# Every large SBUF tile starts at a multiple of 512 bytes: a two-layer encoder on one Trainium2 core

## The chip, the cores and the metric

One core of one Trainium2 chip runs the whole program. The metric is the device time of one execution in microseconds (us). Three executions of the kernel before took 2646.51, 2648.54 and 2650.86 us; the median, 2648.54 us, is the time before. Engines are named as in the profile: PE multiplies matrices, PEld loads its stationary operand, DVE and ACT work on vectors, POOL is a slower helper, and SP issues nearly all DMAs.

## The reference

Two groups of tokens (512 and 256, together T = 768 columns) pass through the same two layers and a final RMSNorm, all in float32 with D = 1024:

```python
x = x + 0.5 * swiglu(rmsnorm(x, f1_n), f1_g, f1_u, f1_d)      # 1024 -> 2816 -> 1024
x = x + mixer(rmsnorm(x, mix_n), ...)                         # layer 0: gated MLP beside windowed
...                                                           # attention; layer 1: 2-D neighbourhood attention
x = x + 0.5 * swiglu(rmsnorm(x, f2_n), f2_g, f2_u, f2_d)
```

So there are six phases: l0f1, l0m, l0f2, l1f1, l1m, l1f2. The four feed-forward phases (FFNs) take three quarters of the time.

## The kernel before

**How a product is made.** Activations lie transposed: 128 features on the partitions, tokens along the row. Each float32 operand is split into a high and a low float32r part, and `mm3` (L175) adds three matmuls in PSUM: high by high, low by high, high by low. All of PE's matmuls of this kind are recorded at L139 in `mmul`. Weights arrive as `raw` tiles of 128 rows of 4,096 bytes (`raw`, L91, issued by SP), and `wsplit` (L103) makes `whi` on ACT (L113) and `wlo` on DVE (L114). `whi` and `wlo` are then the stationary operand, 128 columns at a time; the activation tile (`b11` to `b22`, `d`, `xh`, `xl`, `oh`, `ol`) is the moving operand, mostly 384 columns of 4 bytes, so 1,536 bytes in each partition. In the profile a matmul stands as `ps<-moving,stationary`.

**An FFN.** `ffn` (L416) uses Strassen's scheme on halves of the tokens and of the features, with seven products in place of eight. The gate and up products of a pair of 128 hidden features are 7 products x 2 names x 4 slices x 3 = 168 matmuls that move the `b11`, `b21`, `t1`, `t2`, `t3`, `n4`, `b22` tiles (I call them b tiles; 56 of them, in the pool `comb`). There are 11 pairs: 1,848 such matmuls for each FFN. `down` (L628) multiplies the hidden features back: 84 matmuls for a pair that move `db`, `dt`, `dn` tiles, and `down_last` (L693) another 192 with `dh` (d tiles, in the pool `work`). The order of PE is written out by hand; the other engines follow a scheduler with semaphores for each tile.

**Where tiles lie.** A partition of SBUF has 229,376 bytes. Tiles are placed when the program is built: sizes are padded to 32 bytes, and a pool opened on the left or right side grows from that end. On the left end, in bytes: 2,176 are taken before the program's own tiles; `ident`, `ones`, `onesr` 3 x 512; `gains`, `ngains` 2 x 224; eight `x` tiles of 3,072; four `raw` of 4,096; ten `whi`/`wlo` of 2,048; `acc` 3,072; three `nt` of 1,536; and the norms' small tiles `sm`, `smi`, `yh`, `yl`, together 480. So `x`, `raw`, `whi`, `wlo`, `acc` and `nt` all start 64 bytes past a multiple of 512, and the first tile of the left side stands at 73,760 = 144 x 512 + 32. The right side ends at 229,344 = 447 x 512 + 480. The big pools follow in tiles of 1,536, 2,048 or 3,072 bytes, all multiples of 512. So **every b, d, xh, xl, oh or ol tile that lies on the left starts 32 past a multiple of 512, and on the right 480 past one.**

The side changes with the phase (`open` L80, `other` L771, `mixer_tiles` L774, `ffn_open` L303):

| phase | stretch of the profile, us | b tiles or xh, xl, oh, ol | d tiles |
|---|---|---|---|
| l0f1 | 0 to 523 | right (480) | left (32) |
| l0m | 523 to 782 | right (480) | - |
| l0f2 | 782 to 1283 | left (32) | right (480) |
| l1f1 | 1283 to 1772 | left (32) | right (480) |
| l1m | 1772 to 2132 | left (32) | - |
| l1f2 | 2132 to 2647 | right (480) | left (32) |

Counted in the built program, 11,980 matmuls move 384 columns over all 128 rows: 5,880 from a start of 480 with a stationary operand at 64, 5,880 from 32 with one at 64, 96 from 480 with one at 480, 96 from 32 with one at 32 (the last two are `dh` with the kept weights `khi`, `klo`), and 28 others. Another 2,216 move 256 or 512 columns over 128 rows, in the mixers, from starts of 32, 64, 448 or 480.

Of the kernel before, what the change touches and what calls it, by code (L numbers as in the profile page):

```python
# [9 lines left out]
F32 = mybir.dt.float32  # L10
F32R = mybir.dt.float32r
BF16 = mybir.dt.bfloat16
I32 = mybir.dt.int32
# [3 lines left out]
P = 128  # L17
D = 1024
KD = D // P
# [9 lines left out]
NORMS = ("l0_ffn1_norm", "l0_mix_norm", "l0_ffn2_norm", "l1_ffn1_norm", "l1_mix_norm", "l1_ffn2_norm", "final_norm")  # L29
# [9 lines left out]
NMASK = 8 * (24 + 32 + 24) + 4 * (40 + 40)  # L39
# [12 lines left out]
class Trunk:  # L52
# [4 lines left out]
    def __init__(self, ctx, tc, aps, phases=PHASES):  # L57
        self.tc, self.nc, self.aps, self.phases = tc, tc.nc, aps, phases
        self.units = []
        self.woff = self.pi = 0  # L60
        self.t = 0.0
        self.chains = []
        self.spare = []
        self.first = []
        self.copied = []
        pool = lambda name, bufs, **kw: ctx.enter_context(tc.tile_pool(name=name, bufs=bufs, **kw))
        self.cp = pool("const", 1)
        self.xp = pool("x", 1)
        self.rawp = pool("raw", 4)
        self.wp = pool("w", NW)  # L70
        self.np_ = pool("norm", 1)
        self.mm = pool("mm", 4, space=bass.MemoryType.PSUM)
        self.aux = pool("aux", 4, space=bass.MemoryType.PSUM)
        self.dram = pool("spill", 1, space=bass.MemoryType.DRAM)
        self.guards = {}
        self.side = "left"
# [147 lines left out]
    def norm_tok(self, acc, c0, c1):  # L224

        nb = (c1 - c0) // P
        ps = self.psum(self.aux, "aux")
        for b in range(nb):
            self.mmul(ps[:, b : b + 1], acc[:, c0 + b * P : c0 + (b + 1) * P], self.ones[:, 0:1], True, True)
        sm = self.np_.tile([P, 3, 6], F32, tag="sm", name="sm", bufs=3)  # L230
        it = self.np_.tile([P, 6], I32, tag="smi", name="smi", bufs=2)
        y = sm[:, 1, :nb]
        self.rsqrt(y, ps[:, :nb], 1.0 / D, sm[:, 0, :nb], sm[:, 2, :nb], it[:, :nb])
        return y

    def norm_spread(self, y, pool=None):

        nc = self.nc
        yh = self.np_.tile([P, 3], F32R, tag="yh", name="yh", bufs=2)
        yl = self.np_.tile([P, 3], F32, tag="yl", name="yl", bufs=2)  # L240
        nc.vector.tensor_copy(yh, y)
        nc.vector.tensor_tensor(out=yl, in0=y, in1=yh.bitcast(F32), op=ALU.subtract)
        rb = self.psum(self.aux, "aux")
        for i, t in enumerate((yh.bitcast(F32), yl)):
            diag = (
                pool.tile([P, H], F32R, tag="diag", name="diag", bufs=2)
                if pool and i
                else self.np_.tile([P, H], F32R, tag="nt", name="diag", bufs=3)
            )
            for b in range(3):  # L250
                c = slice(b * P, (b + 1) * P)
                if i:
                    nc.scalar.activation(diag[:, c], self.ident, AF.Copy, scale=t[:, b : b + 1])
                else:
                    nc.vector.tensor_scalar(
                        out=diag[:, c], in0=self.ident, scalar1=t[:, b : b + 1], scalar2=None, op0=ALU.mult
                    )
            self.mmul(rb[:, :H], self.onesr, diag, i == 0, i == 1)
        return rb[:, :H]
# [637 lines left out]
    def finish_rows(self, pool, n, ps_list, outs, adds, init, sink=None):  # L897


        nc = self.nc  # L900
        st = pool.tile([P, 4, 8], F32, tag="st", name="st", bufs=3)
        mx, nm, sm, ri = (st[:, i, :] for i in range(4))
        for i in range(n):
            nc.vector.tensor_tensor_reduce(  # L904
                out=outs[i], in0=ps_list[i], in1=adds[i], scale=1.0, scalar=init[i],
                op0=ALU.add, op1=ALU.max, accum_out=mx[:, i : i + 1],
            )
        nc.vector.tensor_scalar(out=nm[:, :n], in0=mx[:, :n], scalar1=-1.0, scalar2=None, op0=ALU.mult)  # L908
        for i in range(n):
            nc.scalar.activation(  # L910
                outs[i], outs[i], AF.Exp, bias=nm[:, i : i + 1], accum_out=sm[:, i : i + 1]
            )
        if sink is not None:
            nc.vector.tensor_tensor(out=ri[:, :n], in0=sink, in1=nm[:, :n], op=ALU.add)
            nc.scalar.activation(ri[:, :n], ri[:, :n], AF.Exp)
            nc.vector.tensor_tensor(out=sm[:, :n], in0=sm[:, :n], in1=ri[:, :n], op=ALU.add)
        nc.vector.reciprocal(ri[:, :n], sm[:, :n])
        for i in range(n):
            nc.vector.tensor_scalar(  # L919
                out=outs[i], in0=outs[i], scalar1=ri[:, i : i + 1], scalar2=None, op0=ALU.mult  # L920
            )


    def mixer0(self):
        nc = self.nc
        mp = self.mixer_open("m0")
# [7 lines left out]
                nc.sync.dma_start(t[:, c0:c1], self.aps["rope"][i, :, : c1 - c0])  # L934
        msk = mp.tile([P, 3 * P], F32, tag="msk", name="msk")
        nc.sync.dma_start(msk, self.aps["gmask"])
        sink = mp.tile([P, 8], F32, tag="sink", name="sink")
        nc.sync.dma_start(sink, self.aps["sink"].partition_broadcast(P))
        lng = mp.tile([P, 512], F32, tag="lng", name="lng")
        nc.sync.dma_start(lng, self.aps["ln_g"].partition_broadcast(P))  # L940
# [231 lines left out]
    def mixer1(self):  # L1172
        nc = self.nc
        mp = self.mixer_open("m1")
# [1 line left out]
        xs = (self.xh, self.xl)  # L1176
        self.xcols = lambda k, c0, c1: (self.xh[k][:, c0:c1], self.xl[k][:, c0:c1])
        TE = TA + 64
        mb = mp.tile([P, NMASK], BF16, tag="mb", name="mb")
        for i in range(0, NMASK, 512):  # L1180
            n = min(512, NMASK - i)
            mf = mp.tile([P, 512], F32, tag="tb", name="mf")
# [224 lines left out]

    def build(self):
        nc = self.nc
        self.ident = self.cp.tile([P, P], F32, tag="ident", name="ident")  # L1410
        make_identity(nc, self.ident)
        self.ones = self.cp.tile([P, P], F32, tag="ones", name="ones")
        nc.gpsimd.memset(self.ones, 1.0)
        self.onesr = self.cp.tile([P, P], F32R, tag="onesr", name="onesr")
        nc.vector.tensor_copy(self.onesr, self.ones)
        self.gains = self.cp.tile([P, KD * len(NORMS)], F32, tag="gains", name="gains")
        nc.scalar.dma_start(self.gains, self.aps["gains"])
        self.ngains = self.cp.tile([P, KD * len(NORMS)], F32, tag="ngains", name="ngains")
        nc.gpsimd.tensor_scalar(out=self.ngains, in0=self.gains, scalar1=-1.0, scalar2=None, op0=ALU.mult)
        self.x = [self.xp.tile([P, T], F32, tag=f"x{m}", name=f"x{m}") for m in range(KD)]  # L1420
        todo = [KIND[p] for p in self.phases] + [("last", 6)]
        kind = todo[0][0]
        if kind == "f":
            self.ffn_open("right")
            self.ffn_tiles()
            self.fw = self.open("work", "left")
        elif kind != "last":
            self.mixer_tiles("right")
        self.norm_begin(todo[0])
        for h, (c0, c1) in enumerate(HALVES):  # L1430
            for m in range(KD):
                nc.sync.dma_start(self.x[m][:, c0:c1], self.aps["x"][m, :, c0:c1])
                if not (h and kind == "f"):
                    self.final(m, c0, c1)
                if h == 0 and m % 4 == 3 and kind == "f":
                    pre = f"{self.phases[0][:2]}_ffn{self.phases[0][3]}"
                    self.first += [self.raw(f"{pre}_w_{n}", 0, KD, m // 4 * 2 * P, P) for n in ("gate", "up")]
            if h and kind == "f":
                self.spawn(self.second())
            elif kind in ("f", "last"):  # L1440
                self.half_done(h)
            if kind == "last":
                self.drain()
        for i, ph in enumerate(self.phases):
            self.following = todo[i + 1]
            if i == 0 and "l1m" in self.phases:
                self.bias_tables()
            if ph == "l1m":
                while self.spare:
                    self.spare.pop(0)()  # L1450
            if ph == "l0m":
                self.mixer0()
            elif ph == "l1m":
                self.mixer1()
            else:
                self.ffn(f"{ph[:2]}_ffn{ph[3]}")
        self.drain()
        for n in list(self.guards)[::-1]:
            self.close(n)
# [103 lines left out]
```

## Time and profile before

| | |
|---|---|
| runs | 2646.51, 2648.54, 2650.86 us, median 2648.54 |
| span of the profiled execution (first to last instruction) | 2646.8 us |
| DVE busy | 2272.7 us (86%) |
| ACT busy | 1369.5 us (52%) |
| POOL busy | 87.9 us (3%) |
| DMA | 218.99 MB, mean 83 GB/s |

No run time of the profiled execution stands apart from its span, so what lies around the span is taken as the median less the span, 1.7 us. In the views below, "the chain" is the chain of work that ended last, followed back from the last instruction; a row of it gives a start, a length, the engine with what it writes, and how many instructions are merged. A matmul's duration in the profile includes its pipelined end, so what one costs in a row of matmuls is read from the distance between starts, or from a chain row's length divided by its count.

### The profile page before, as it was taken

The page shows a single profiled execution, that of the slowest core. Times are in us where ns is not written, and L with a number is a line of the kernel's source. Part 1 is how long each engine was busy: PE and PEld are TensorE (multiplying, and loading weights), DVE is VectorE, ACT ScalarE, POOL GpSimd, SP SyncE. Part 2 cuts the span into 40 slices and gives each one's busy share as a digit, 9 for nine tenths or more (in the row PEclk, how much of TensorE's full clock was granted, in tenths as well). Part 3 has the DMA queues.
Part 4 walks back from the last instruction along what each step waited for, and adds up shares of the span by engine and source line. Part 5 has one row for each costly group of instructions (what it writes and reads, how often), then busy time and mean ns, then how long its engine had stood idle before and what let it go on. Part 6 is the DMA issues. An engine that isn't in the chain of part 4 may idle for free.

```text
span 2646.8 us, 41176 instructions
## 1 busy us (share of the span) xinstructions
PE 2576.9 (97%) x15094; PEld 2505.0 (95%) x15094; DVE 2272.7 (86%) x4793; ACT 1369.5 (52%) x2851; POOL 87.9 (3%) x172
## 2 busy tenths in 40 slices
PE   7999999998999999999999999999999999999997
PEld 7999999987899999999999999989898999999997
DVE  8998889889769988898999888886677699988886
ACT  7544444555656544445654544454455465454443
POOL 0000000000100000000000000002222100000000
PEclk9999999999999999999999999999999999999999
DMA  5323222431222222222222221232221332222221
GB/s 173 127 83 91 76 79 66 133 98 37 86 74 100 80 80 65 80 72 88 96 80 80 64 80 65 84 119 65 63 63 40 104 104 80 80 72 72 70 83 56
DMA packets 83898, 218.99 MB, mean 83 GB/s; under 512 B 20080, under 2 KB 32880, under 8 KB 83696
## 3 DMA queue, kind: packets, MB, share of 16 engines
q1 hardware_dynamic: 83552, 216.34, 25.4%
q8 instruction: 118, 1.93, 0.3%
q14 instruction: 84, 0.69, 0.1%
q10 hardware_dynamic: 144, 0.03, 0.0%
HBM read 206.90 MB, written 15.07 MB: 84 GB/s over the span
## 4 chain that ended last, share of the span: by engine, by line
PE 88%; DVE 7%; ACT 2%; DMA 1%; issue 1%; SPq 0%; DVEq 0%; ACTq 0%
PE ps_mm L139 55%; PE ps_aux L139 32%; DVE wlo L114 1%; DMA raw<-in_w 1%; PE ps_aux L143 1%; ACT p L910 1%; DVE xl L738 1%; ACT whi L113 0%; DVE p L919 0%; DVE tl L196 0%; DVE p L904 0%; DVE s L608 0%; ACT xh L737 0%; DVE ol L196 0%; DVE x L705 0%
## 5 line engine op out<-in xcount | busy, mean ns | idle before, releaser
L113 ACT CAST whi<-s 128x512 fp32r<-128x512 f32 x496 | 305.4, 622 | 396.3 <-DVE s L608 142.8
L113 ACT CAST whi<-raw 128x512 fp32r<-128x512 f32 x512 | 312.3, 621 | 265.6 <-PE ps_mm L139 119.5
L114 DVE TENSOR_TENSOR wlo<-s,whi 128x512 fp32r<-128x512 f32 x496 | 338.3, 688 | 71.0 <-ACT whi L113 70.6
L114 DVE TENSOR_TENSOR wlo<-raw,whi 128x512 fp32r<-128x512 f32 x494 | 339.5, 695 | 26.7 <-ACT whi L113 23.8
L139 PE MATMUL ps_aux<-dt,whi 128*128 128x384 f32 x864 | 222.7, 339 | 2.1 <-ACT whi L113 2.1
L139 PE MATMUL ps_mm<-db,whi 128*128 128x384 f32 x864 | 221.6, 338 | 0.0
L139 PEld LDWEIGHTS ps_aux<-dt,whi 128*128 128x128 f32 x864 | 157.6, 189 | 2.4 <-ACT whi L113 2.4
L139 PEld LDWEIGHTS ps_mm<-db,whi 128*128 128x128 f32 x864 | 156.8, 188 | 0.0
L139 PE MATMUL ps_mm<-xh,whi 128*128 128x512 f32 (+1 forms) x416 | 147.5, 355 | 4.0 <-ACT xh L737 4.0
L139 PE MATMUL ps_aux<-dt,wlo 128*128 128x384 f32 x432 | 146.7, 340 | 0.2 <-DVE wlo L114 0.2
L139 PE MATMUL ps_mm<-db,wlo 128*128 128x384 f32 x432 | 146.1, 338 | 0.0
L139 PE MATMUL ps_mm<-xl,whi 128*128 128x512 f32 (+1 forms) x416 | 142.5, 343 | 1.1 <-DVE xl L738 1.1
L139 PE MATMUL ps_mm<-xh,wlo 128*128 128x512 f32 (+1 forms) x416 | 142.2, 342 | 0.0
L498 DVE TENSOR_TENSOR u<-ps_aux,u 128x384 f32<-128x384 f32 x176 | 97.6, 555 | 4.2 <-PE ps_aux L139 3.5
L608 DVE TENSOR_TENSOR s<-raw,raw 128x512 f32<-128x512 f32 x124 | 83.9, 688 | 18.1 <-DMA raw<-in_w 18.1
L139 PE MATMUL ps_aux<-dh,whi 128*128 128x384 f32 x384 | 98.4, 338 | 0.7 <-DVE x L705 0.7
L608 DVE TENSOR_TENSOR s<-raw 128x512 f32<-128x512 f32 x124 | 85.4, 690 | 14.2 <-DMA raw<-in_w 13.7
L910 ACT ACTIVATE p<-p,st 128x256 f32<-128x256 f32 (+3 forms) x144 | 69.1, 483 | 54.8 <-DVE st L908 54.6
L660 DVE TENSOR_TENSOR x<-ps_aux,x 128x384 f32<-128x384 f32 x160 | 86.6, 554 | 11.8 <-PE ps_aux L139 11.8
L493 ACT COPY u<-ps_mm 128x384 f32<-128x384 f32 x176 | 83.7, 476 | 24.6 <-PE ps_mm L139 24.5
L139 PE MATMUL ps_mm<-oh,whi 128*128 128x384 f32 x256 | 89.2, 348 | 4.6 <-DVE x L887 4.0
L139 PEld LDWEIGHTS ps_mm<-xh,whi 128*128 128x128 f32 x416 | 79.4, 191 | 14.6 <-ACT xh L737 4.9
(486 smaller groups left out, 8092.4 us busy)
## 6 DMA issues: line engine op xcount, KB each, us to landing
raw<-in_w SPq DMA_DIRECT2D x350, 512.0 KB, 3.6
xdm<-x SPq DMA_DIRECT2D x16, 384.0 KB, 2.3
x<-in_x SPq DMA_DIRECT2D x16, 192.0 KB, 5.7
x<-xdm SPq DMA_DIRECT2D x8, 384.0 KB, 3.3
xold<-xdm SPq DMA_DIRECT2D x8, 384.0 KB, 3.0
out_y<-y SPq DMA_DIRECT2D x8, 384.0 KB, 2.5
tab<-skew SPq DMA_DIRECT2D x8, 256.0 KB, 5.0
raw<-in_w SPq DMA_DIRECT2D x8, 256.0 KB, 2.6
```

Source lines behind the costliest of these rows:

```text
L113: nc.scalar.copy(hi, src)
L114: (eng or nc.gpsimd).tensor_tensor(out=lo, in0=src, in1=hi.bitcast(F32), op=ALU.subtract)
L139: self.nc.tensor.matmul(out, lhsT=lhsT, rhs=rhs, start=start, stop=stop, **kw)
L143: self.nc.tensor.transpose(out, src, self.ident)
L493: nc.scalar.copy(e[n, out], bank[key, n])
L498: nc.vector.tensor_tensor(out=t, in0=bank[key, n], in1=t, op=ALU.add)
L608: f = lambda o, x, y, op: self.nc.vector.tensor_tensor(out=o, in0=x, in1=y, op=op)
L660: nc.vector.tensor_tensor(out=o, in0=ps, in1=o, op=ALU.add)
L738: nc.vector.scalar_tensor_tensor(out=lo, in0=src, scalar=gain, in1=hi.bitcast(F32), op0=ALU.mult, op1=ALU.subtract)
L910: nc.scalar.activation(outs[i], outs[i], AF.Exp, bias=nm[:, i : i + 1], accum_out=sm[:, i : i + 1])
```

## The change

No operation is added or taken away. A tile `space` of 384 bytes fills the left end up to 2,560 = 5 x 512, `gains` and `ngains` grow to 256 bytes each, and the small tiles of the norms go to a pool at the right end, where their 480 bytes bring the right side's end to 228,864 = 447 x 512. In the mixers the `st` tiles (128 bytes) are four and not three, `sink` takes 512 bytes, and `mb` 2,048 and not 1,920. Afterwards all 11,980 matmuls of 384 columns over 128 rows, and the 2,216 of 256 and 512, have both the moving and the stationary operand at a multiple of 512. Some tiles still do not start there, among them `vhh` and `vhl` behind the small tiles of the gating (192 past) and the `add` tiles of the neighbourhood bias.

Instruction by instruction, the order on every engine is the same in both programs, and so is what each instruction waits for, but for three loads of the bias tables (L1190) on SP: one load of `ba` and one of `bb` lose a wait for PE, and an earlier `bb` takes over the first of these waits.

```diff
@@ __init__
         self.np_ = pool("norm", 1)
+        self.sp = pool("small", 1, side="right")
@@ norm_tok, norm_spread
-        sm = self.np_.tile([P, 3, 6], F32, tag="sm", name="sm", bufs=3)
-        it = self.np_.tile([P, 6], I32, tag="smi", name="smi", bufs=2)
+        sm = self.sp.tile([P, 3, 6], F32, tag="sm", name="sm", bufs=3)
+        it = self.sp.tile([P, 6], I32, tag="smi", name="smi", bufs=2)
...
-        yh = self.np_.tile([P, 3], F32R, tag="yh", name="yh", bufs=2)
-        yl = self.np_.tile([P, 3], F32, tag="yl", name="yl", bufs=2)
+        yh = self.sp.tile([P, 3], F32R, tag="yh", name="yh", bufs=2)
+        yl = self.sp.tile([P, 3], F32, tag="yl", name="yl", bufs=2)
@@ finish_rows
-        st = pool.tile([P, 4, 8], F32, tag="st", name="st", bufs=3)
+        st = pool.tile([P, 4, 8], F32, tag="st", name="st", bufs=4)
@@ mixer0
-        sink = mp.tile([P, 8], F32, tag="sink", name="sink")
+        sink = mp.tile([P, P], F32, tag="sink", name="sink")[:, :8]
@@ mixer1
-        mb = mp.tile([P, NMASK], BF16, tag="mb", name="mb")
+        mb = mp.tile([P, NMASK + 64], BF16, tag="mb", name="mb")
@@ build
+        self.cp.tile([P, 96], F32, tag="space", name="space")
         self.ident = self.cp.tile([P, P], F32, tag="ident", name="ident")
...
-        self.gains = self.cp.tile([P, KD * len(NORMS)], F32, tag="gains", name="gains")
+        self.gains = self.cp.tile([P, 64], F32, tag="gains", name="gains")[:, : KD * len(NORMS)]
...
-        self.ngains = self.cp.tile([P, KD * len(NORMS)], F32, tag="ngains", name="ngains")
+        self.ngains = self.cp.tile([P, 64], F32, tag="ngains", name="ngains")[:, : KD * len(NORMS)]
```

## The prediction

> **What bounds the kernel now.** I read the page first (its busy shares, clock and chain), then the chain in order of time, then stretches, and last single instructions.
>
> ```profile
> span 2646.8 us, 41176 instructions
> ...
> PE 2576.9 (97%) x15094; PEld 2505.0 (95%) x15094; DVE 2272.7 (86%) x4793; ACT 1369.5 (52%) x2851; POOL 87.9 (3%) x172
> ...
> PEclk9999999999999999999999999999999999999999
> ...
> PE 88%; DVE 7%; ACT 2%; DMA 1%; issue 1%; SPq 0%; DVEq 0%; ACTq 0%
> ```
>
> PE is busy for 97% of the span at a granted clock of 0.9 or more in every slice, and it makes 88% of the chain. So what a matmul costs in a row of matmuls is what the kernel costs. The change alters no operation and no order; it alters addresses. The question is therefore narrow: does any engine's time depend on where its operands start, and is there anything in the profile before, where three or four starts occur, that tells? The chain in order of time does. Its columns are start, length, and the merged matmuls.
>
> ```profile
> 267.23 8.32 PE ps_aux L139 x48
> ...
> 743.23 26.54 PE ps_mm L139 x153
> ...
> 951.80 16.64 PE ps_mm L139 x96
> ...
> 976.76 20.80 PE ps_mm L139 x120
> ...
> 1014.27 8.48 PE ps_mm L139 x48
> ...
> 2191.43 12.72 PE ps_mm L139 x72
> ...
> 2300.75 16.96 PE ps_mm L139 x96
> ...
> 2326.19 21.20 PE ps_mm L139 x120
> ```
>
> The rows at 951.80 and 976.76 (l0f2, b tiles on the left, start 32) and those at 2300.75 and 2326.19 (l1f2, b tiles on the right, start 480) are the same products of the same code. On the left 96 take 16.64 us, 173.3 ns each, and 120 take 20.80, again 173.3. On the right they take 16.96 and 21.20: 176.7 ns, 3.33 ns or 1.9% more. The d tiles have the sides exchanged: 48 at 267.23 (left) take 8.32 us, 173.3 each, and 48 at 1014.27 (right) 8.48, 176.7. It is not the phase that is slow, then, but the tile's side. Stretches of two pairs (rows one, two, three, four) and of one `down` (rows five, six) say the same; the columns are the stretch, its length, and busy time and count of PE, PEld, DVE, ACT, POOL, then clock and DMA.
>
> ```profile
> 191.00:250.20 59.20, 59.20 (x337) 59.20 (x336) 50.14 (x90) 28.70 (x57) 0.00 (x0) 1.00 0.35 106
> 951.60:1009.70 58.10, 58.10 (x337) 58.10 (x336) 51.98 (x94) 29.43 (x58) 0.00 (x0) 1.00 0.24 73
> 1444.90:1502.90 58.00, 58.00 (x336) 58.00 (x335) 51.81 (x94) 29.37 (x58) 0.00 (x0) 1.00 0.23 73
> 2300.60:2359.80 59.20, 59.20 (x337) 59.20 (x337) 52.45 (x95) 29.66 (x59) 0.00 (x0) 1.00 0.21 72
> 1009.90:1039.40 29.50, 29.50 (x169) 29.50 (x168) 25.00 (x47) 12.94 (x26) 0.00 (x0) 1.00 0.24 72
> 2271.50:2300.40 28.90, 28.90 (x168) 28.90 (x167) 26.50 (x51) 13.32 (x26) 0.00 (x0) 1.00 0.23 74
> ```
>
> For 336 matmuls the right side takes 59.20 us and the left 58.00 or 58.10, with PE busy all the time, DVE idle for 6 us or more in each of them, the clock at 1.00 and the DMA share as high on the fast side (0.24 against 0.21). Neither a wait, nor the clock, nor DMA traffic makes the difference. Single starts show its form: the first three rows are of l0f2, the others of l1f2.
>
> ```profile
> 976.60 0.34 PE L139 MATMUL ps_mm<-n40h,whi 128*128 128x384 f32 x1
> 976.77 0.34 PE L139 MATMUL ps_mm<-n40l,whi 128*128 128x384 f32 x1
> 976.94 0.34 PE L139 MATMUL ps_mm<-n40h,wlo 128*128 128x384 f32 x1
> ```
> ```profile
> 2326.02 0.34 PE L139 MATMUL ps_mm<-n40h,whi 128*128 128x384 f32 x1
> 2326.20 0.34 PE L139 MATMUL ps_mm<-n40l,whi 128*128 128x384 f32 x1
> 2326.38 0.34 PE L139 MATMUL ps_mm<-n40h,wlo 128*128 128x384 f32 x1
> 2326.56 0.34 PE L139 MATMUL ps_mm<-n41h,whi 128*128 128x384 f32 x1
> ```
>
> On the right three starts in a row come 0.54 us after the first where the even pace would give 0.52: about every second matmul slips by some 6 ns. I call such a stretch slipping.
>
> But a start of 480 doesn't always slip. The chain's row at 743.23 is l0m's output projection, with `oh` and `ol` on the right: 153 in 26.54 us, 173.5 ns. So 480 seems to allow two paces, of which one is held once it has set in; in FFN stretches from 32 I find no lasting slip. That limits what can be argued, and it comes back under the rivals.
>
> **The change part by part.**
>
> *Moving operands on the right, 480 to 0.* How many slip? In each of l0f1 and l1f2, three blocks of 336 b matmuls and a last half one of 168 run at the pace of rows one and four above; by their difference of 1.1 us for 336 the 1,176 cost 3.9 us, so 7.8 us in both. Earlier in these phases PE still waits in between and only part slips (the 72 at 2191.43 do: 12.72 us, 176.7 ns): some 200 in l0f1 and 430 in l1f2, by the chain's pieces, x 3.33 ns = 2.1 us. The d matmuls of l0f2 and l1f1 on the right: 756 each, 1,512 x 3.33 ns = 5.0 us (the two `down` stretches above differ by 0.6 us for 168, or 3.6 ns each, the same size). About 155 of `dh` in l1f1 add 0.5 us. Together 4,650 matmuls and 15.4 us.
>
> Does 0 keep the pace of 32, or that of 480? No matmul of 384 columns starts there before. What can be compared: an operand that starts 480 past a multiple of 512 has 32 bytes up to that multiple, one at 32 has 480, one at 0 has all 512; the order speaks for 0 behaving like 32 or better. I take 173.3 ns. The bounds are: from below, 12 thousand matmuls at 1.5 ns less than that (the 256-column rows under the rivals); from above, every one at the slipping pace.
>
> *Moving operands on the left, 32 to 0, and stationary ones, 64 to 0.* At 173.3 ns these stand at the best pace that the trace has for 384 columns, and I cost them at nothing. That both operands then have the same offset has a precedent: `dh` with the kept weights, 480 with 480, in l0f2. Its first and its following row:
>
> ```profile
> 1244.52 0.51 PE L139 MATMUL ps_aux<-dh,khi 128*128 128x384 f32 x2
> ...
> 1252.86 0.34 PE L139 MATMUL ps_aux<-dh,whi 128*128 128x384 f32 x1
> ```
>
> Between them lie 48 matmuls in 8.34 us: 173.8 ns, no slip to speak of. If it did matter, 5,880 matmuls on the left by up to 3.33 ns would be +19.6 us.
>
> *DVE and ACT.* The same casts and subtractions occur with sources on either alignment: `s` lies on the sides (32 or 480), `raw` at 64.
>
> ```profile
> L113 ACT CAST whi<-s 128x512 fp32r<-128x512 f32 x496 | 305.4, 622 | 396.3 <-DVE s L608 142.8
> L113 ACT CAST whi<-raw 128x512 fp32r<-128x512 f32 x512 | 312.3, 621 | 265.6 <-PE ps_mm L139 119.5
> L114 DVE TENSOR_TENSOR wlo<-s,whi 128x512 fp32r<-128x512 f32 x496 | 338.3, 688 | 71.0 <-ACT whi L113 70.6
> L114 DVE TENSOR_TENSOR wlo<-raw,whi 128x512 fp32r<-128x512 f32 x494 | 339.5, 695 | 26.7 <-ACT whi L113 23.8
> ```
>
> 622 against 621 ns on ACT; on DVE 688 against 695, the wrong way round for a cost of odd starts. Nothing is taken. If DVE gained the 7 ns on its 990 rows of L114, that is 7 us of an engine that idles 6 us in 58 under PE's cover; if it lost as much the cover still holds.
>
> *DMA.* Rows of `raw` move from 64 to 0. Loads stand behind PE's work all through the FFNs; in the open they lie at the start, where the chain's longest DMA piece is this one:
>
> ```profile
> 2.60 5.04 DMA raw<-in_w
> ```
>
> No load of before lands at 0 past 512, so its price is bounded by nothing and by all that could reasonably vanish: I take 0, with 1 us either way. The Trainium skill ("DMA: Bandwidth & Descriptors", How a descriptor splits into AXI transactions) says that a piece not starting on a 256-byte boundary needs one transaction more; a row of 4,096 bytes would take 17 and not 16, and by that an estimated 0.3 us of these 5.04 would go. No trace here shows it.
>
> *The moved waits.* Three `ba`/`bb` loads wait differently, at about 1779 us. Behind them on SP come the other bias loads and a weight load. Who needs them is POOL:
>
> ```profile
> 1785.17 2.97 POOL L1197 TENSOR_TENSOR add<-ba,mb 128x192 f32<-128x192 f32 x4 [12.61 <-DVE mb L1184]
> ```
>
> It starts at 1785.17, released by the mask `mb` on DVE, not by these loads; a wait for PE that ends a few matmuls sooner or later stays under that. Nothing. The fourth `st` tile, the larger `sink`, `mb` and `gains` change no wait at all.
>
> *The sum.* 15.4 us of matmul time. In the full blocks PE never waits and all of it reaches the end; in the first 100 us and at the seams of phases it waits for DVE and ACT, where I leave out 0.9 us. What is late next is DVE with 52 of 58 us, so nothing catches it. 2646.8 - 14.5 = 2632.3 us of span; with 1.7 us around it, **2634 us**, 0.55% under the median of the three runs.
>
> **The rivals.**
>
> *No change.* The slip is a matter of phase between PE and its operand stream, and the address only happens to go with it: for this speaks the row at 743.23, a start of 480 without a slip; against it, that every one of the full blocks on the right slips and none on the left, with b and d tiles changing sides. The time is then 2648.5 us. The Trainium skill ("SBUF — State Buffer", Specifications (TRN2)) gives lines of 16 bytes as what an operand is fetched by; all starts before are multiples of 32, so by it nothing would be gained. The rows at 951.80 and 2300.75 differ although both starts are whole such lines, so the trace doesn't follow it here.
>
> *Slower.* With both streams at 0, the moving and the stationary operand reach each multiple of 512 together, and every stretch of 384-column matmuls slips. It would show in the FFNs on the side that was clean, rows like 951.80 going from 16.64 to 16.96. The price: about 7,300 of the 11,980 don't slip now; if they slip in the proportion in which those on the right do, 4,650 of 5,880 or 79%, 9,460 slip, 4,810 more than now: +16.0 us, 2664 us. If all do, +24.4 us. It decides as soon as more than 4,650 of 11,980, 39%, slip. For it: no row has 0; a slip does occur in one offset of four or so. Against: the 48 `dh` matmuls with equal offsets keep 173.8 ns.
>
> *Faster still.* Starts of 32 and 480 both leave a fetch that is cut by a boundary, and a whole one is cheaper than either. The 256-column rows of l1m and l0m hint at it:
>
> ```profile
> L139 PE MATMUL ps_mm<-xl,whi 128*128 128x256 f32 x208 | 58.4, 281 | 0.0
> L139 PE MATMUL ps_mm<-xh,wlo 128*128 128x256 f32 x208 | 58.4, 281 | 0.0
> ...
> L139 PE MATMUL ps_mm<-wlo,xh 128*128 128x256 f32 x192 | 53.7, 280 | 0.0
> L139 PE MATMUL ps_mm<-whi,xl 128*128 128x256 f32 x192 | 53.6, 279 | 0.0
> ```
>
> With `xh` or `xl` moving (32 or 480) one takes 281 ns, with `whi` or `wlo` moving (64) 279 or 280. 1.5 ns on 11,980 matmuls would be 18 us more, 2616 us. Against it: the even 173.3 ns everywhere from 32 looks like a floor, and these operands have changed roles as well.
>
> **How the numbers follow.** The forecast, 2634 us (2629 to 2640 with its own unknowns), has a chance of 0.55: the side effect is plain, but 0 itself is not in the trace. Faster still, about 2616: 0.09. No change: 0.17. Slower, about 2664: 0.19. The range of 80% takes in the forecast, no change with its spread, and part of the faster case: 2618 to 2658 us. A measurement can tell about 0.2% from no change, 5.3 us: below 2643.2 us lie the forecast and the faster case, 0.64; within it no change, 0.17; above it 0.19.
>
> **What would show it.** In the chain of after, l1f2's pieces of 96 and 120 should read 16.64 and 20.80 us, as l0f2's do, and d pieces of 48 8.32 in all four FFNs; the stretches of 336 should take 58.0 to 58.1 us everywhere. DVE's and ACT's 622 and 688 to 695 ns should stand. The forecast is wrong if l0f2's pieces grow (slower), if l1f2's stay at 16.96 (no change), if any of them falls under 16.6 (faster still), or if PE's gain is there and a wait for DVE eats it.

## The result and the profile after

Five runs of the changed kernel took 2630.94 to 2637.34 us, median **2634.87 us**; five runs of the kernel before on the same chip took 2646.51 to 2650.86, median 2648.76. The ratio is **0.9944** with a 95% interval of [0.9932, 0.9956]: 14 us less. The forecast was 2634. The time came out as predicted; the reason that the prediction gave for it did not hold, and most of what follows is about that. As in the prediction, a row of matmuls *slips* when one takes more than the even 173.3 ns; a row at 173.3 ns I call *clean*.

The page of after, first its span, then busy time by engine, the clock by slices and the chain's shares:

```profile
span 2633.1 us, 41175 instructions
...
PE 2561.3 (97%) x15094; PEld 2491.3 (95%) x15094; DVE 2267.8 (86%) x4793; ACT 1365.6 (52%) x2851; POOL 88.0 (3%) x172
...
PEclk9999999999999999999999999999999999999998
```

PE is busy 15.6 us less (2576.9 before) for the same 15,094 matmuls at the same clock, and the span is 13.7 us shorter. So the matmuls gained 15.6 us, and on balance 1.9 us were given back as waits. The chain of work that ended last shows where (start, length, engine and tile, merged matmuls; lines stand one further down than in before, so L140 is L139 there):

```profile
736.87 26.54 PE ps_mm L140 x153
...
942.01 16.64 PE ps_mm L140 x96
...
966.98 20.80 PE ps_mm L140 x120
...
1004.41 8.32 PE ps_mm L140 x48
...
2290.85 16.64 PE ps_mm L140 x96
...
2315.81 20.80 PE ps_mm L140 x120
```

The row at 2290.85 is the one that took 16.96 us in before (at 2300.75), the one at 2315.81 took 21.20, and the d piece at 1004.41 took 8.48. All are now at 173.3 ns for each matmul, what l0f2's b tiles had before and keep (942.01, 966.98). l0m's output projection (736.87) has its 26.54 us in both.

### The profile page after: what moved, and what is told of

The parts are those of the page before. It is cut to its first block, busy times and chain, and to the rows that moved or that the text cites. A ratio compares the mean times of both kernels' runs of the same rounds, so it can differ in the third digit from the quotient of the medians.

```text
span 2633.1 us, 41175 instructions
## 1 busy us (share of the span) xinstructions
PE 2561.3 (97%) x15094; PEld 2491.3 (95%) x15094; DVE 2267.8 (86%) x4793; ACT 1365.6 (52%) x2851; POOL 88.0 (3%) x172
## 4 chain that ended last, share of the span: by engine, by line
PE 86%; DVE 9%; ACT 2%; DMA 2%; issue 1%; SPq 0%; DVEq 0%; ACTq 0%
PE ps_mm L140 54%; PE ps_aux L140 31%; DMA raw<-in_w 1%; DVE wlo L115 1%; PE ps_aux L144 1%; DVE s L609 1%; DVE xl L739 1%; ACT p L911 1%; DVE p L920 0%; DVE p L905 0%; DVE tl L197 0%; ACT whi L114 0%; ACT xh L738 0%; DVE ol L197 0%; DVE x L706 0%
## 5 line engine op out<-in xcount | busy, mean ns | idle before, releaser
L140 PE MATMUL ps_aux<-dt,whi 128*128 128x384 f32 x864 | 219.3, 334 | 2.1 <-ACT whi L114 2.1
L140 PE MATMUL ps_mm<-db,whi 128*128 128x384 f32 x864 | 219.2, 334 | 0.0
L140 PEld LDWEIGHTS ps_aux<-dt,whi 128*128 128x128 f32 x864 | 156.0, 188 | 2.4 <-ACT whi L114 2.4
L140 PEld LDWEIGHTS ps_mm<-db,whi 128*128 128x128 f32 x864 | 156.1, 188 | 0.0
L140 PE MATMUL ps_mm<-xh,whi 128*128 128x512 f32 (+1 forms) x416 | 147.4, 354 | 3.8 <-ACT xh L738 3.8
L140 PE MATMUL ps_aux<-dt,wlo 128*128 128x384 f32 x432 | 144.4, 334 | 0.3 <-DVE wlo L115 0.3
L140 PE MATMUL ps_mm<-db,wlo 128*128 128x384 f32 x432 | 144.4, 334 | 0.0
L140 PE MATMUL ps_mm<-xl,whi 128*128 128x512 f32 (+1 forms) x416 | 142.3, 342 | 1.1 <-DVE xl L739 1.1
L140 PE MATMUL ps_mm<-xh,wlo 128*128 128x512 f32 (+1 forms) x416 | 142.1, 341 | 0.0
L140 PE MATMUL ps_aux<-dh,whi 128*128 128x384 f32 x384 | 97.6, 335 | 0.6 <-DVE x L706 0.6
L140 PEld LDWEIGHTS ps_mm<-xh,whi 128*128 128x128 f32 x416 | 79.9, 192 | 14.1 <-ACT xh L738 4.9
L140 PE MATMUL ps_mm<-oh,whi 128*128 128x384 f32 x256 | 88.1, 344 | 4.6 <-DVE x L888 4.0
```

Of the source, the lines that this page charges most:

```text
L140: self.nc.tensor.matmul(out, lhsT=lhsT, rhs=rhs, start=start, stop=stop, **kw)
```

## The experiments

The prediction's reason is theory **START**: where the moving operand starts decides, and a start of 480 slips. The rival that I set beside it, **DISTANCE**: the start of the moving operand less that of the stationary one decides; before, this was 480 - 64 = 416 on the right and 32 - 64, or 480, on the left (distances are taken modulo 512). The change made both zero at once, so its own trace cannot tell the two apart. I write starts as moving/stationary: before has 480/64 on the right and 32/64 on the left, after 0/0.

**1 to 3: one operand at a time.** Unused filler tiles shift one side or both.

```diff
 # e1_right_only: the kernel before, right side at 0
+        self.sp = pool("small", 1, side="right")
+        self.sp.tile([P, 120], F32, tag="fill", name="fill")
 # e2_right_480: the kernel after, right side back at 480
         self.sp = pool("small", 1, side="right")
+        self.sp.tile([P, 8], F32, tag="fill", name="fill")
 # e3_both_480: as e2, and the left side at 480 too
+        self.np_.tile([P, 120], F32, tag="left", name="left")
```

> The kernel before, with 480 unused bytes at the right end: the tiles of the right side start at 0 past a multiple of 512, those of the left stay at 32, the weights stay at 64. Theory START (a matmul slips by where its moving operand starts; 480 slips, 0 and 32 do not): nearly the whole gain, 2633 to 2637 us, and the chain's pieces of 96 at 16.64 us in all four FFNs. Rival DISTANCE (it slips by how far the moving start lies from the stationary one, modulo 512; 416 slips, 480 and 0 do not): the distance is now 448, which no row has; if that slips the time stays at 2648 us.

> The changed kernel, with 32 unused bytes at the right end: the right side starts at 480 again, while the left side and the weights stay at 0. START: the slip is back on the right, 15 us of matmul time, 2646 to 2652 us, pieces of 96 in the last FFN at 16.96 us. DISTANCE: the distance is 480, as it was for the clean left side before, so no slip and about 2635 us.

> The changed kernel with both sides at 480 and the weights at 0. START: some 80% or all of the 11,980 matmuls of 384 columns slip by 3.33 ns, 2664 to 2675 us, pieces of 96 at 16.96 us in all FFNs. DISTANCE: 480 everywhere, no slip, about 2635 us.

Measured: e1 2638.55 us, ratio to before 0.9956 [0.9944, 0.9968]; e2 2635.42 us, 0.9943 [0.9932, 0.9955]; e3 2636.28 us, 0.9949 [0.9936, 0.9961]. The chain of e2, where the b tiles of l1f2 are at 480 as they were in before:

```profile
2291.28 16.65 PE ps_mm L141 x96
...
2316.25 20.80 PE ps_mm L141 x120
```

and of e3, where every moving operand of the FFNs is at 480:

```profile
2289.64 16.64 PE ps_mm L142 x96
...
2314.60 20.80 PE ps_mm L142 x120
```

e1 shows that the right side alone carries most of the gain. Its 2638.55 us lie 1.6 us above the upper end of what START expected, while DISTANCE had left open what 448 does. Some rows do slip there, although 0 should be clean by START: l0m's output projection, at 0/64, took 26.54 us in before and after, and in e1

```profile
737.42 27.04 PE ps_mm L141 x153
```

e2 and e3 tell the theories apart: the same start of 480 that took 16.96 us beside weights at 64 takes 16.64 or 16.65 beside weights at 0. **START falls.**

**4: starts alone.** The kernel does nothing of the encoder, only rows of matmuls on zeros (its output is left zero): 96 of 384 columns at each of 16 moving starts, with the stationary operand at 0 and at 64, then 48 each of 256 and 512 columns.

```diff
+        for s in (0, 64):
+            for o in offs + [0]:
+                group(f"c384s{s}o{o}z", o, s, 32, 384, mm)
+        for o in offs:
+            group(f"c256s0o{o}z", o, 0, 16, 256, mm)
+        for o in offs:
+            group(f"c512s0o{o}z", o, 0, 16, 512, mm)
```

> Matmuls alone, with nothing of the encoder computed (the output is left at zero): one moving and one stationary tile, groups of 96 matmuls of 384 columns with the moving start at 0, 32, ... 480 past a multiple of 512 and the weights at 0 and then at 64, and groups of 48 with 256 and with 512 columns. No other engine works beside them. START: 173.3 ns at 0 and 32, 176.7 at 480, the same with weights at 0 and at 64; the starts between tell where the border lies. DISTANCE: with weights at 64 the pattern is moved by 64 against that with weights at 0. If other engines' accesses make the slip, no group slips.

It took 869.78 us. Groups of matmuls by costliest line; `s` is the stationary start, `o` the moving one, then busy us and mean ns, which includes the pipelined end:

```profile
L1432 PE MATMUL c384s64o160z<-mov,sta 128*128 128x384 f32 x96 | 17.1, 339 | 0.0
...
L1432 PE MATMUL c384s0o96z<-mov,sta 128*128 128x384 f32 x96 | 17.1, 339 | 0.0
L1432 PE MATMUL c384s0o352z<-mov,sta 128*128 128x384 f32 x96 | 17.1, 339 | 0.0
L1432 PE MATMUL c384s0o128z<-mov,sta 128*128 128x384 f32 x96 | 17.1, 338 | 0.0
...
L1432 PE MATMUL c384s64o192z<-mov,sta 128*128 128x384 f32 x96 | 17.1, 338 | 0.0
...
L1432 PE MATMUL c384s0o160z<-mov,sta 128*128 128x384 f32 x96 | 16.8, 336 | 0.0
...
L1432 PE MATMUL c384s64o480z<-mov,sta 128*128 128x384 f32 x96 | 16.8, 336 | 0.0
...
L1432 PE MATMUL c384s64o128z<-mov,sta 128*128 128x384 f32 x96 | 16.8, 336 | 0.0
```

With weights at 0 the starts 96, 128, 352 and 384 slip; with weights at 64 the starts 160, 192, 416 and 448. The pattern moves with the weights by exactly 64, and repeats after 256: distances of 96 and 128 slip, modulo 256. A distance of 192, or 448 as in e1, isn't clean either: in the chain 0/64, first behind 0/0 and later behind 480/64, takes 176.7 and then 174.7 ns for each matmul.

```profile
313.17 16.96 PE c384s64o0z L1432 x96
...
581.10 16.77 PE c384s64o0z L1432 x96
```

DISTANCE is right in kind. (Nearly every group here follows the one with the start 32 lower, so this run alone doesn't separate the distance from what ran ahead.) But before's own pair 480/64, a distance of 416 or 160 modulo 256, stands at 16.8 here (and so does 160/0). Alone, it did not slip; in the FFNs it did. Something was still missing.

**5 to 7: only the weights move.**

```diff
 # e5_weights_96: the kernel after; in bytes, gap 96 and gap2 416
 # (e6_weights_384: after, 384 and 128; e7_weights_480: before, 416 and 96)
+        self.gap = pool("gap", 1)
+        self.gap.tile([P, 24], F32, tag="gap", name="gap")
         self.wp = pool("w", NW)
+        self.gap2 = pool("gap2", 1)
+        self.gap2.tile([P, 104], F32, tag="gap2", name="gap2")
```

> The kernel after with only the whi and wlo tiles moved, from 0 to 96 past a multiple of 512; every moving operand stays at 0. Distance theory (the start of the moving operand less that of the stationary one decides): the distance is 416 for 11,760 matmuls of 384 columns, the one that the right side had before, now on both sides. Slips return in every FFN although the moving operand is at 0: pieces of 96 at 16.96 us wherever the matmuls run on, l0f2 too, which never slipped. 11,760 x 3.33 ns = 39.2 us if all slip, 31 us if four in five do: 2666 to 2674 us. Rival (each operand's own alignment decides, and before it was the moving operand's start of 480): 2635 us, pieces of 96 at 16.64.

> The kernel after with only the whi and wlo tiles moved, from 0 to 384 past a multiple of 512, so that every start is a multiple of 128. Distance theory: the distance is 128 for 11,760 matmuls of 384 columns, which slipped in the run of matmuls alone; all slip, also behind waits: 2635 + 39 = 2674 us, pieces of 96 at 16.96 us. Rival (own alignment): 2635 us, pieces at 16.64, since 384 is as round a start as any.

> The kernel before with only the whi and wlo tiles moved, from 64 to 480 past a multiple of 512; all moving operands stay where they were, 480 on the right and 32 on the left, so that not one matmul of 384 columns has an operand at a multiple of 512. Distance theory: distances 0 and 64, neither slips: the whole gain of the change without any aligned tile, 2633 to 2638 us, pieces of 96 at 16.64 us in l1f2. Rival (own alignment): 2648 us or more, pieces of 96 at 16.96 in l1f2 as before.

Measured: e5 2641.9 us, 0.9976 [0.9966, 0.9985]; e6 2662.53 us, 1.0046 [1.0034, 1.0058]; e7 2633.02 us, 0.9935 [0.9922, 0.9948].

e7 has the whole gain with no FFN operand at a multiple of 512, as DISTANCE expected. e6 has every start at a multiple of 128 and is 28 us slower than after, where 39 were expected: all rows slip, but by less. Its chain in l1f2:

```profile
2314.17 16.85 PE ps_mm L144 x96
...
2339.45 21.07 PE ps_mm L144 x120
```

16.85 us for 96 is 175.5 ns: at a distance of 128 the slip is 2.2 ns and not 3.3. Over all rows of at least 24 it is 2.5 ns; x 11,760 that is 29 us.

e5 is the miss. It has before's slipping distance, 416, on both sides, and neither 2666 to 2674 nor 2635 came out. Its chain, first in l0f1:

```profile
71.81 8.48 PE ps_aux L144 x48
80.29 12.72 PE ps_mm L144 x72
```

and further on, in l0f2 and l1f2:

```profile
946.27 16.64 PE ps_mm L144 x96
...
2187.15 12.72 PE ps_mm L144 x72
...
2298.17 16.64 PE ps_mm L144 x96
```

The same starts, 0/96, run at 176.7 ns in one stretch and at 173.3 in another. From the time between starts, in rows of at least 24 matmuls, some 1,050 run at 176.7 ns and some 10,000 at 173.4; the slipping ones lie near the start of three FFNs, between 67 and 144 us, between 822 and 873, and between 2173 and 2246. So 416 allows both paces, and a row holds the one that it has. That is what the prediction had seen at 743.23 and left standing.

**8: what came ahead.** Again matmuls alone, on zeros. First, groups of 384 at four pairs of starts, with nothing beside them (`cn`), with DVE (`cd`), ACT (`ca`) or both at work; then 96 at 480/64, each behind 24 at another moving start (`from32` is behind 32/64) or behind a wait for DVE.

```diff
+        for kind in ("", "d", "a", "da"):
+            for s, o in ((0, 0), (64, 32), (64, 480), (0, 128)):
+                beside(kind)
+                group(f"c{kind or 'n'}s{s}o{o}z", o, s, 128, 384, mm)
+        for o in offs:
+            group(f"p{o}z", o, 64, 8, 384, mm)
+            group(f"from{o}z", 480, 64, 32, 384, mm)
+        for i in range(6):
+            nc.vector.tensor_copy(a, raw[:, :3712])
+            group(f"wait{i}z", 480, 64, 32, 384, mm)
```

> Matmuls of 384 columns alone, in groups of 384, with nothing, DVE, ACT or both working beside; then groups of 96 at moving 480 and stationary 64 (distance 416), each behind 24 matmuls of another moving start, or behind a wait for DVE. It computes nothing of the encoder (the output is zeros). Question: distance 416 slips in the FFNs but not in l0m's output projection and not in the earlier run of matmuls alone. Theory A (what comes ahead decides: the pace is taken over at entry and held): the group at 480 that directly follows one at 32 slips, 176.7 ns, with or without work beside, and among the groups behind 16 starts some slip throughout and some not at all. Theory B (work on DVE or ACT beside it sets it off): 173.3 ns with nothing beside, 176.7 with DVE, ACT or both, and all groups behind other starts at 173.3. Both expect 173.3 at 0 on 0 and at 32 on 64, and 176.7 at 128 on 0, whatever is beside.

It took 1561.4 us. Groups by line:

```profile
L1432 PE MATMUL cns64o480z<-mov,sta 128*128 128x384 f32 x384 | 68.0, 340 | 0.0
...
L1432 PE MATMUL cns0o128z<-mov,sta 128*128 128x384 f32 x384 | 67.6, 338 | 0.0
...
L1432 PE MATMUL cdas64o480z<-mov,sta 128*128 128x384 f32 x384 | 66.7, 336 | 0.0
...
L1432 PE MATMUL cns64o32z<-mov,sta 128*128 128x384 f32 x384 | 66.7, 336 | 0.0
L1432 PE MATMUL cns0o0z<-mov,sta 128*128 128x384 f32 x384 | 66.7, 334 | 0.0
...
L1432 PE MATMUL from64z<-mov,sta 128*128 128x384 f32 x96 | 17.1, 340 | 0.0
...
L1432 PE MATMUL from32z<-mov,sta 128*128 128x384 f32 x96 | 17.1, 340 | 0.0
...
L1432 PE MATMUL from0z<-mov,sta 128*128 128x384 f32 x96 | 16.8, 337 | 0.0
...
L1432 PE MATMUL from96z<-mov,sta 128*128 128x384 f32 x96 | 16.8, 336 | 0.0
```

`cns64o480z` follows directly on 384 matmuls at 32/64 and slips throughout with DVE and ACT idle: 68.0 us, 1.3 more than its neighbour. Theory B, that work beside it is needed, falls. (With work beside it the group at 480/64 runs clean at 66.7; but there a single matmul at 0/0 stands ahead of it, so this doesn't show that the work helps.) Of the 16 groups behind other starts, eight slip at 17.1 us and eight don't: behind 32, 64, 192, 224 and these plus 256 they slip, behind 0, 96, 128, 160 and these plus 256 they don't. Behind waits, between starts, four settle at 173.3 ns and two at 176.7. At 128/0 all four groups slip (67.6 or 67.7 us), whatever comes ahead. So: at a distance of 0 or 32/64's 480 a row of matmuls is clean, at 128 it slips, and at 416 what ran ahead sets the pace in which it begins, and it holds that. Theory A, **HISTORY**, fits in this. But the pace isn't taken over from the row ahead: by the time between starts, the 24 at 32/64 run at 173.7 ns and the group behind them slips, the 24 at 160/64 run at 176.5 and the group behind them doesn't.

**9 and 10: history in the kernel itself.** It makes two odd forecasts: spoil the left side of before, and the untouched right side runs clean; give after a right side at 416, and it slips as in before.

```diff
 # e9_left_480: the kernel before, left side from 32 to 480
+        self.np_.tile([P, 112], F32, tag="left", name="left")
 # e10_right_416: the kernel after, right side from 0 to 416
+        self.sp.tile([P, 24], F32, tag="fill", name="fill")
```

> The kernel before with an unused 448-byte tile on the left, so that its b and d tiles there start at 480 and not at 32; the right side and the weights (64) are untouched. All 11,760 matmuls of 384 columns now have the distance 416 of before's right side. History theory (at 416 the pace of what came ahead is kept; before, each change from 32 to 480 put PE into the slow one): without that change the slow pace is entered only now and then, so the untouched right side is freed as well: 2638 to 2646 us, l1f2's pieces mostly 96 in 16.64 us. Side or start theory (a stretch at 480 against 64 in a long row slips by itself): everything slips, 2648 + 16 to 24 = 2664 to 2672 us, pieces of 96 at 16.96 on both sides.

> The kernel after with an unused 96-byte tile in the pool at the right end, so that the right side starts at 416; the left side and the weights stay at 0. Distances 0 on the left and 416 on the right, changing with every pair. History theory: each change from distance 0 to 416 enters the slow pace, as the group behind a start equal to the weights' did in the run of matmuls alone; the right side slips as in before, pieces of 96 in l1f2 at 16.96 us, 2635 + 14 = 2646 to 2651 us. Rival (416 is slow only now and then whatever came ahead, as with the weights at 96): 2636 to 2643 us.

Measured: e9 2637.28 us, 0.9963 [0.9951, 0.9976], a little under the lower end of what was expected; e10 2650.16 us, 1.0001 [0.9992, 1.0011]. The chain of e9 in l1f2, whose b tiles and weights have the starts of before, 480/64:

```profile
2289.06 16.64 PE ps_mm L140 x96
...
2314.02 20.80 PE ps_mm L140 x120
```

and of e10, with l0m and l0f2 ahead of l1f2:

```profile
742.50 27.04 PE ps_mm L141 x153
...
951.59 16.64 PE ps_mm L141 x96
...
1014.08 8.48 PE ps_mm L141 x48
...
2302.22 16.96 PE ps_mm L141 x96
...
2327.66 21.20 PE ps_mm L141 x120
```

In e9 none of the 11,063 matmuls at 480/64 in long rows slips, and those on the right lie on the very addresses that slipped in before. In e10 4,872 of 5,505 at 416/0 slip at 176.7 ns, in the places where before slipped and also in l0m's output projection (742.50), which didn't in before; its left side, 0/0, is clean. In before, 4,504 of 5,532 at 480/64 did, and part of a row of 96. Both e5 and e10 have the distance 416; one changes between 0 and 416 with every pair and slips, the other stays at 416 and mostly doesn't.

## Why the prediction was right in its time and wrong in its reason

- **The matmuls' gain.** 4,650 slipping matmuls and 15.4 us were forecast; in rows of at least 24, 4,504 slipped and part of 96 more, and PE's busy time fell by 15.6 us. A block of 336 went from 59.36 us (by before's chain, at 176.7 ns) to 58.24 by after's, at 173.3. This step was right in count and price, because both were read from before's own rows.
- **The step that failed** is "an operand that starts 480 past a multiple of 512 has 32 bytes up to that multiple ... the order speaks for 0 behaving like 32 or better", with "not the phase that is slow, then, but the tile's side" before it. No boundary of 512 matters: 480 beside weights at 0 is clean (e2, e3), and 416 beside 0, further from the boundary, slips (e10). What the rows of before showed was a side together with a distance together with a change of distance in front of it. 0 behaved like 32 because both distances, 0 and 480, are of the clean kind. That a wrong reason gave the right pace was in part luck: by the same reason 0 beside weights at 384 would be clean, and it costs 28 us (e6).
- **Edits costed at nothing.** The weights' move from 64 to 0 was one of them, at "the best pace that the trace has". By itself a move of the weights is worth the whole gain (e7: 64 to 480) or a loss of 28 us against after (e6: 0 to 384). The cost at the final pair of starts came out right; that the edit does nothing was wrong. The left side's move from 32 to 0 is at 173.3 ns before and after, as said.
- **The Trainium skill** ("TensorE: Matmul & The Clock Gate", Step-by-step: what each phase is for) gives PE two independent read ports, one for the moving operand and one for the weights, so that loading the next weights takes nothing from the running matmul. By that the weights' start should not matter to the matmuls, but with it alone moved, 96 of them take 16.64 us (after) or 16.85 (e6). Whether the two operands meet at the ports or elsewhere, no run shows.
- **The rival "slower"** saw both streams at 0 meet at each boundary: not so, 0/0 is clean throughout (`cns0o0z`, 66.7 us for 384). But its price, 2664 us, is about that of e6, where the distance is 128. Had the change chosen such starts, that rival would have come true. Before's trace has no row at 128. It has one at 0, the 48 `dh` with `khi` that the prediction set against this rival (173.8 ns): of its arguments for the final starts this is the one that the runs bear out.
- **No change** rested on the row at 743.23. Its reading, that one pair of starts allows two paces of which one is held, was right; that the change would then do nothing was not, since 0/0 has only the clean pace.
- **Faster still** rested on 256 columns. They went the other way, and 512 columns gained. Of before and then of after, groups by line with shapes kept apart:

```profile
L139 PE MATMUL ps_mm<-xl,whi 128*128 128x512 f32 x208 | 84.1, 404 | 1.1 <-DVE xl L738 1.1
```
```profile
L140 PE MATMUL ps_mm<-xl,whi 128*128 128x512 f32 x208 | 83.5, 402 | 1.1 <-DVE xl L739 1.1
...
L140 PE MATMUL ps_mm<-xl,whi 128*128 128x256 f32 x208 | 58.8, 283 | 0.0
```

  512 columns take 402 ns (404), 256 columns 283 (281 and 279). In the mixers these two nearly cancel.
- **DVE and ACT.** 688 and 695 ns were expected to stand, as was 622. After's groups:

```profile
L115 DVE TENSOR_TENSOR wlo<-raw,whi 128x512 fp32r<-128x512 f32 x494 | 337.5, 691 | 28.3 <-ACT whi L114 24.1 <-PE ps_mm L140 0.4
L115 DVE TENSOR_TENSOR wlo<-s,whi 128x512 fp32r<-128x512 f32 x496 | 337.0, 685 | 61.1 <-ACT whi L114 60.8
```
```profile
L114 ACT CAST whi<-s 128x512 fp32r<-128x512 f32 x496 | 304.9, 621 | 390.6 <-DVE s L609 133.1 <-PE ps_mm L140 118.1 <-issue 74.6
```

  They stand within 4 ns, and what changed is under PE's cover.
- **DMA and the seams.** 0.9 us was left out for the waits, 1.9 went. The first load was longer, which alone is 1.0 us, at the edge of the 1 us that was allowed:

```profile
2.62 6.06 DMA raw<-in_w
```

  The address doesn't account for it: in the profiled executions of the kernels with `raw` at 0 (after, e2, e3, e5, e6, e10) this row read 5.08 to 6.30 us, and with `raw` at 64 (before, e1, e7, e9) 5.04 to 6.12. The rest is a balance. By the same matmuls in both traces, after loses 1.7 us of its lead between 1283 and 1357 us and 2.2 between 2132 and 2178, at the starts of l1f1 and l1f2, and gains 1.6 between 770 and 790, at the end of l0m. In l1f1 the chain of after passes through loads where before's has only PE, one of them

```profile
1308.69 5.07 DMA raw<-in_w
```

  One could think that a faster PE comes to these seams before the weights do, but the other runs don't bear it out. For the same matmuls in l1f1 before takes 73.9 us and after 75.7, but e7, as clean as after, 74.0. In l1f2 before takes 45.9 and after 48.1, but e2, as clean as after, 45.9, and e10, which slips like before, 47.8. What makes these stretches longer or shorter stays open.

## What to carry to other kernels

When two stretches of the same matmuls differ by an address, write down both operands' starts, and what ran ahead of the stretch, before naming the address that matters; one filler tile in front of one pool tells them apart. Rounding everything to 512 was one way of several to a clean pair here: moving only the weights did as much, and another round number, 384, cost 28 us. A gain read from the rows of the stretches that will vanish can be right in size though its reason is wrong, so a right time is no proof of the reason.

## What the runs showed of the hardware that I had not expected

- 384-column matmuls with a weight load each run at 173.3 ns or slip, by the moving start less the stationary start modulo 256: distance 0 clean wherever it stood (66.7 us for 384), 96 slipping in all four groups of the fourth experiment (17.1 us for 96 against 16.8), 128 slipping wherever it stood (175.5 to 176.0 ns), 160 in two paces, 173.3 or 176.7 ns, of which a row holds the one in which it begins, and 192 in several: 174.7 and 176.7 ns in the fourth experiment, 176.7 (l0m) and 173.3 (l1f2) in e1.
- Shapes want different distances. With the weights at 0, alone:

```profile
L1432 PE MATMUL c512s0o32z<-mov,sta 128*128 128x512 f32 x48 | 11.4, 395 | 0.0
...
L1432 PE MATMUL c512s0o0z<-mov,sta 128*128 128x512 f32 x48 | 11.1, 390 | 0.0
...
L1432 PE MATMUL c256s0o0z<-mov,sta 128*128 128x256 f32 x48 | 5.9, 283 | 0.0
...
L1432 PE MATMUL c256s0o32z<-mov,sta 128*128 128x256 f32 x48 | 5.8, 279 | 0.0
```

  At distance 0 and at 256, which is 0 modulo 256, 512 columns are quickest (389 and 390 ns against up to 396) and 256 columns slowest (283 against 279 to 282).
- Open: what in PE makes the two streams meddle with each other, why `480/64` was clean in the fourth experiment behind 448/64 and slipped in the eighth behind the same, why l0m's output projection at a distance of 416 is clean in before and slips in e10, and the half of e5's 7 us over after that its slipping rows (1,050 x 3.33 ns = 3.5 us) leave unexplained.
